# Ten gate tiles moved into the seven-product stage, and the recurrence's setup in longer vector operations

## The chip, the core and the metric

The kernel runs on one core of one Trainium2 chip. The core has five engines with an instruction queue each: PE (TensorE, matmuls), DVE (VectorE), ACT (ScalarE), POOL (GpSimd) and SP (SyncE, which here only starts transfers). They run side by side and wait for each other by semaphores. The metric is the device time of one execution in microseconds, and the median of the runs is what counts.

## What is computed

One layer of a streaming encoder on 512 positions (L) of 2048 channels (D), all in float32:

```
h = rmsnorm(x, norm_g)
[v, bg, cg, za | u, zb | ga, gb] = h @ w_in          # 4x2048 | 2x1024 | 2x2048 columns
ya = bg * causal_conv3(cg * v);   ya = (ya * silu(za)) @ w_out_a
yb = gelu(s5_scan(u, ...));       yb = yb * sigmoid(yb @ w_glu + b_glu)
yb = (yb * silu(zb)) @ w_out_b
m  = sigmoid(ga) * ya + sigmoid(gb) * yb
out = rmsnorm(x + m @ w_o, final_g)
```

`s5_scan` is a diagonal complex recurrence: 64 groups of 16 channels, 64 states each, with a per-state decay that is worked out from a_re, a_im and log_dt.

## The kernel before

**Float32 on PE.** A weight w is split into a rounded w_hi (a cast on ACT, line 544) and w_lo = w - w_hi (a subtraction on DVE, line 561); an activation is held as the same kind of pair. `WStream` loads the weights (128x1024 at a time, w_raw, on SP) some steps ahead and keeps four w_hi and four w_lo buffers. A plain `gemm` is 8 k-steps of three matmuls 128x512: hi times hi, hi times lo, lo times hi (lines 696 to 698), 24 matmuls. An output tile of 128 channels by 512 positions needs two gemms (2048 input channels).

**Stages.** (1) u, the recurrence's input, seven tiles at once (to 98.6 us). (2) The gate stage: tiles of ga, gb and zb, two gemms each, and beside them, as background work, the recurrence. (3) `glu` and w_out_b, and two further ga tiles. (4) The seven-product stage: cg, v, za and bg, two tiles at a time. `seven` multiplies 2x2 blocks (two tiles by two halves of the positions) with seven products instead of eight, a `product` being 8 k-steps of one matmul of 512 columns (line 922) and one of 256 (line 924). Its sums of weights are made by `add7` on DVE. (5) Two last ga tiles, then w_out_a, then w_o. The gates go through tanh on ACT (line 823) and are parked in DRAM (ga_d, gb_d) by POOL until stage 5.

**Background work.** `bg` is a list of generators. `gemm(..., steps=RATE)` advances the list by RATE steps after each gemm. In the gate stage the list holds the recurrence's parameters, then four `Block`s (16 of the 64 groups each), then eight gelu pieces. A Block has a `front` (factors f for every power, small matrices bb, and sl, made by DVE and ACT), `pe1` (float32 matmuls on PE that need sl, line 338, and bb with f, line 347), `post` (mi, el), `scan` on DVE (seven doublings that make the rotations rr and ri, then a turn of h, a scan of 16 instructions at line 415, and a turn back) and `pe2` (matmuls of h with el, lines 430 and 433). `ssm_blocks` runs them in the order front 0, then for each block pe1, pe2 of the block before, post, front of the next, scan.

**What sets the order.** The code is written in one stream. A scheduler then puts each engine's instructions into one fixed queue, and an engine runs its queue in order.

In the changed code the numbers of these lines are 1 to 3 higher, so that line 823 appears as L826 in the order rows of the change, 544 as L545, 561 as L562, 338 as L339, 433 as L434, 325 (sl) as L326.

Of the kernel before, what the change touches and what calls it, by code (L numbers as in the profile page):

```python
# [12 lines left out]
AF = mybir.ActivationFunctionType  # L13
ALU = mybir.AluOpType
ADD, SUB, MUL = ALU.add, ALU.subtract, ALU.mult

P = 128
L = 512
D = 2048
KD = D // P  # L20
NG, NP, NC = 64, 64, 16
NQ = NG // 2
NB = 4
QB = NQ // NB
T = 4
# [1 line left out]
SLOT = 1024  # L27
EPS = 1e-6
MAGIC = 12582912.0
RATE = 2.75  # L30
PRATE = 1.0
WARM = 9
NR4 = 37
NA = 12
NAB = 14
HL = L // 2


# [198 lines left out]
class Block:  # L237
# [13 lines left out]
    def front(self):  # L251
        c, nc, b, q0, msk = self.c, self.c.nc, self.b, self.q0, self.msk
        tt, ts, stt = _ew(nc)
# [19 lines left out]
        cr, ci = smal[:, :, 1, 0, :], smal[:, :, 1, 1, :]  # L273
        shp = [P, QB, NC]
        ft = self.new([P, QB, 5, NC], "ft")
        for ri in range(2):
            f = self.new([P, QB, 5, NC], "f")
            for tau in range(5):
                pr = c.pw[:, tau, 0, q0:q0 + QB].unsqueeze(2).to_broadcast(shp)
                pi = c.pw[:, tau, 1, q0:q0 + QB].unsqueeze(2).to_broadcast(shp)  # L280
                tt(ft[:, :, tau, :], ci, pi if ri == 0 else pr, MUL)
                tt(f[:, :, tau, :], cr, pr if ri == 0 else pi, MUL)
                if tau == 2:
                    yield
            if ri == 0:
                tt(f, f, ft, SUB)
            else:
                fl = f.rearrange("p q t c -> p (q t c)")
                stt(fl, fl, -1.0, ft.rearrange("p q t c -> p (q t c)"), MUL, SUB)
            self.F.append(f)  # L290
            yield
# [21 lines left out]
        tmp = self.new([P, QB, 2, NP], "t")  # L313
        for ri in range(2):
# [8 lines left out]
            m = self.new([P, QB, 2, NP], "sl")  # L323
# [254 lines left out]
def hybrid_kernel(ctx: ExitStack, tc: tile.TileContext, xT, x, cvec, fg, wu, wu7, wabc,  # L578
                  wgz, wgb, wga, wo, par, bs_d, be_d, ce_d, out):
    nc = tc.nc  # L580
    tt, ts, stt = _ew(nc)
    act = nc.scalar
    c = Ctx()
# [16 lines left out]
    def wide(name, shape=(P, 2, L)):  # L600
        t = r4b.tile(list(shape), F32, tag="r4", name=name)
        return t

    def tmp():
        if r4b:
            return wide("tmp")[:, 0]
        t = tp_ctx.tile([P, L], F32, tag="tmp", name="tmp")
        return t
# [9 lines left out]
    W, W2 = WStream(c, 2, 2), WStream(c, 0, 0)  # L618
# [20 lines left out]
    for j in range(0, KD, 2):  # L639
        for i in range(4):  # L640
            W.add7(wabc[j, i, 0], wabc[j + 1, i, 0], wabc[j + 1, i, 1], wabc[j, i, 1])
    for j in range(NAB, KD):
        for h in range(2):
            W.add(wga[j, h])
    for j in range(KD):
# [25 lines left out]
    ga_d = [drp.tile([P, L], F32, name=f"ga{j}") for j in range(KD)]  # L671
    gb_d = [drp.tile([P, L], F32, name=f"gb{j}") for j in range(KD)]
    tb_d = [drp.tile([P, L], F32, name=f"tb{j}") for j in range(KD)]
    uy = uyp_ctx.tile([P, 8, T, NCH], F32, name="uy")


    bg = []
# [115 lines left out]
    yg = []  # L793

    def gelu(m):
        y = uy[:, m].rearrange("p s k -> p k s")
        t, u = tmp(), tmp()
        t3, u3 = (v.rearrange("p (k s) -> p k s", s=T) for v in (t, u))
        act.activation(t3, y, AF.Square)
        ts(t, t, 0.044715, MUL, 1.0, ADD)  # L800
        tt(t3, t3, y, MUL)
        yield
        act.activation(u, t, AF.Tanh, scale=0.7978845608028654)
        stt(t3, u3, 1.0, y, ADD, MUL)
        g = pair()
        split(g, t)
        yg.append(g)
        yield
# [17 lines left out]

    for j in range(NA):
        gate(ga_d[j], RATE)
    for j in range(KD):
        gate(gb_d[j], RATE)  # L830
    zb = []
    for m in range(8):
# [3 lines left out]
        tz = tmp()  # L836
# [91 lines left out]
    def seven(name):  # L928

        o = wide(name)  # L930
        e1, pb = wide("half"), psum()
        product(pb, Y11, True, False)
        act.copy(e1[:, 0], pb)
        e2, pd = wide("half"), psum()
        product(pd, T1, True, False)
        act.copy(e2[:, 1], pd)
        product(pb, T2, False, False)
        act.copy(e1[:, 1], pb)
        product(pd, Y22, False, True)
        tt(e1[:, 1], pd, e1[:, 1], ADD)  # L940
        product(pb, T3, False, False)
        tt(e2[:, 1], pb, e2[:, 1], ADD)
        pa = psum()
        product(pa, Y21, True, True)
        tt(e1[:, 0], pa, e1[:, 0], ADD)
        for i, e in enumerate((e1, e2)):
            if i:
                product(pb, T4, False, True)
                act.copy(e2[:, 0], pb)
            v = e.rearrange("p b (h l) -> p b h l", h=2)  # L950
            tt(o[:, i].rearrange("p (b l) -> p b l", b=2), v[:, :, 0], v[:, :, 1], ADD)
        return o
# [19 lines left out]
    def out_a(cc, b, j):  # L972
        tt(b, b, cc, MUL)
        nc.gpsimd.dma_start(yag_d[j // 2], b)
        yield

    for j in range(0, KD, 2):
        cc = seven("cg")
        v = seven("v")
        bg.append(conv(cc, v, j))  # L980
        z = seven("za")
        bg.append(silu(cc, z))
        b = seven("bg")
        bg.append(out_a(cc, b, j))
    while bg:
        step()

# [14 lines left out]
        bg.append(reload(i))  # L1002
    for _ in range(3):
        step()
    for j in range(NAB, KD):
        gate(ga_d[j], 4.0)
    while bg:
        step()
# [15 lines left out]
    for j in range(KD):  # L1024
# [4 lines left out]
        t = mq[j]  # L1029
        stt(t[:, 0], t[:, 0], 1.0, ps, ADD, MUL)  # L1030
        stt(t[:, 1], t[:, 1], 0.25, t[:, 0], MUL, ADD)
        p = pair()
# [8 lines left out]
    for t in range(4):  # L1041
        for i in range(2):
            o = c.r4.tile([P, 1024], F32, tag="r4", name="o")
# [45 lines left out]
    for t in range(4):  # L1089
# [16 lines left out]
        v, r, s = (st[:, t, i:i + 1] for i in (5, 6, 7))  # L1106
# [92 lines left out]
```

## Time and profile before

| what | value |
|---|---|
| median of 3 runs | 1708.33 us (1706.68 to 1710.23) |
| the profiled execution | 1708.12 us, of which 1706.3 us are the span of the trace |
| PE busy | 1693.8 us, 99% of the span |
| DVE busy | 1202.0 us, 70% |
| ACT busy | 684.9 us, 40% |
| granted TensorE clock | 0.997 |

The span is the time from the first to the last instruction in the trace; 1.8 us lie around it. A row of a timeline gives the start, the duration, engine, line, operation and tiles, and in brackets how long the engine stood idle before it and what ended that. A row of groups gives the count, the busy time with the mean duration in ns, and the idle time before the group's instructions. The matmuls are pipelined: a duration is longer than the distance to the next start.

### The profile page before, as it was taken

How to read it: one execution, taken by the hardware profiler on the slowest of the kernel's cores; microseconds unless marked ns; L12 is line 12 of the kernel's file. 1: busy time of each engine (PE TensorE's matmuls, PEld its weight loads, DVE VectorE, ACT ScalarE, POOL GpSimd, SP SyncE). 2: the span in 40 equal slices, each digit the busy share in tenths (PEclk: the TensorE clock that was granted, in tenths of full speed). 3: DMA queues.
4: the chain of work that ended last, by engine and by line, in shares of the span. 5: the costliest groups of instructions: out<-in, count | busy, mean ns of one | idle time of the engine just before them, and what ended most of it. 6: DMA issues, size and time to landing. Idle time of an engine off the chain costs nothing.

```text
span 1706.3 us, 21911 instructions
## 1 busy us (share of the span) xinstructions
PE 1693.8 (99%) x8516; PEld 1437.5 (84%) x8516; DVE 1202.0 (70%) x1781; ACT 684.9 (40%) x883; POOL 130.4 (8%) x224
## 2 busy tenths in 40 slices
PE   9999999999999999999999999999999999999997
PEld 7888888888888888888888888888888888888887
DVE  7895483939758677598989889888989644333433
ACT  6434423333326422454545544454545422223221
POOL 0003213040100021000000000000000210000000
PEclk9999999999999999999999999999999999999999
DMA  8323335443441453333333332334334943363212
GB/s 300 112 94 125 111 137 124 139 127 122 149 124 50 165 169 136 111 99 112 99 124 120 117 122 99 112 99 132 114 125 141 349 164 112 111 225 121 74 38 99
DMA packets 65256, 221.96 MB, mean 130 GB/s; under 512 B 8896, under 2 KB 9024, under 8 KB 65152
## 3 DMA queue, kind: packets, MB, share of 16 engines
q1 hardware_dynamic: 49392, 170.94, 29.6%
q0 software_dynamic: 15040, 48.53, 9.1%
q8 instruction: 66, 1.08, 0.3%
q10 hardware_dynamic: 720, 1.10, 0.2%
q14 instruction: 38, 0.31, 0.1%
HBM read 195.24 MB, written 21.10 MB: 127 GB/s over the span
## 4 chain that ended last, share of the span: by engine, by line
PE 98%; DMA 1%; DVE 0%; ACT 0%; SPq 0%; issue 0%; DVEq 0%
PE ps L922 25%; PE ps L698 15%; PE ps L696 15%; PE ps L697 15%; PE ps L924 12%; PE ps L1054 3%; PE ps L1052 3%; PE ps L1053 3%; PE ps L773 1%; PE ps L774 1%; PE ps L775 1%; PE ps L433 1%; PE ps L338 1%; PE ps L347 1%; PE ps L430 0%; DMA w_raw<-in_wu_dram 0%
## 5 line engine op out<-in xcount | busy, mean ns | idle before, releaser
L544 ACT CAST w_hi<-w_raw 128x1024 fp32r<-128x1024 f32 (+2 forms) x341 | 355.8, 1044 | 696.0 <-PE ps L697 352.3
L561 DVE TENSOR_TENSOR w_lo<-w_raw,w_hi 128x1024 fp32r<-128x1024 f32 (+2 forms) x341 | 412.1, 1212 | 310.1 <-ACT w_hi L544 305.9
L696 PE MATMUL ps<-pair,w_hi 128*128 128x512 f32 x1104 | 431.1, 391 | 0.0
L698 PE MATMUL ps<-pair,w_lo 128*128 128x512 f32 x1104 | 429.8, 390 | 0.6 <-DVE w_lo L561 0.6
L697 PE MATMUL ps<-pair,w_hi 128*128 128x512 f32 x1104 | 430.1, 390 | 0.0
L922 PE MATMUL ps<-h_comb,w_hi 128*128 128x512 f32 x1024 | 366.2, 399 | 0.0
L924 PE MATMUL ps<-h_comb,w_lo 128*128 128x256 f32 x1024 | 288.2, 281 | 0.0
L922 PE MATMUL ps<-pair,w_hi 128*128 128x512 f32 x768 | 275.7, 399 | 0.0
L698 PEld LDWEIGHTS ps<-pair,w_lo 128*128 128x128 f32 x1104 | 207.4, 188 | 43.9 <-DVE w_lo L561 1.1
L696 PEld LDWEIGHTS ps<-pair,w_hi 128*128 128x128 f32 x1104 | 207.5, 188 | 42.4
L697 PEld LDWEIGHTS ps<-pair,w_hi 128*128 128x128 f32 x1104 | 207.4, 188 | 42.4
L922 PEld LDWEIGHTS ps<-h_comb,w_hi 128*128 128x128 f32 x1024 | 192.8, 188 | 47.6
L924 PE MATMUL ps<-pair,w_lo 128*128 128x256 f32 x768 | 216.1, 281 | 0.0
L924 PEld LDWEIGHTS ps<-h_comb,w_lo 128*128 128x128 f32 x1024 | 194.0, 189 | 0.0
L922 PEld LDWEIGHTS ps<-pair,w_hi 128*128 128x128 f32 x768 | 144.6, 188 | 35.7
L924 PEld LDWEIGHTS ps<-pair,w_lo 128*128 128x128 f32 x768 | 145.5, 189 | 0.0
L544 ACT CAST w_hi<-w_sum 128x1024 fp32r<-128x1024 f32 x64 | 67.4, 1053 | 104.4 <-PE ps L922 94.1
L561 DVE TENSOR_TENSOR w_lo<-w_sum,w_hi 128x1024 fp32r<-128x1024 f32 x64 | 78.0, 1219 | 7.2 <-ACT w_hi L544 7.2
L1052 PE MATMUL ps<-w_hi,pair 128*128 128x512 f32 (+1 forms) x212 | 81.8, 386 | 0.0
L1053 PE MATMUL ps<-w_lo,pair 128*128 128x512 f32 (+1 forms) x212 | 81.7, 386 | 0.0
L1054 PE MATMUL ps<-w_hi,pair 128*128 128x512 f32 (+1 forms) x212 | 81.7, 386 | 0.0
L47 DVE TENSOR_TENSOR half<-ps,half 128x512 f32<-128x512 f32 x96 | 65.6, 683 | 1.9 <-PE ps L924 1.9
(189 smaller groups left out, 1697.8 us busy)
## 6 DMA issues: line engine op xcount, KB each, us to landing
w_raw<-in_wabc_dram SPq DMA_DIRECT2D x128, 512.0 KB, 3.8
w_raw<-in_wga_dram SPq DMA_DIRECT2D x64, 512.0 KB, 3.6
w_raw<-in_wgb_dram SPq DMA_DIRECT2D x48, 512.0 KB, 4.0
w_raw<-in_wo_dram SPq DMA_DIRECT2D x32, 512.0 KB, 3.3
w_raw<-in_wgz_dram SPq DMA_DIRECT2D x24, 512.0 KB, 3.6
w_raw<-in_wu_dram SPq DMA_DIRECT2D x15, 448.0 KB, 7.7
xt<-in_xT_dram SPq DMA_DIRECT2D x16, 256.0 KB, 6.8
ga<-tmp POOLq DMA_DIRECT2D x16, 256.0 KB, 2.3
```

The costliest lines, as they stand in the source:

```text
L47: return v.tensor_tensor(out=o, in0=a, in1=b, op=op)
L338: nc.tensor.matmul(ps[:, i * NCH:(i + 1) * NCH], self.sl[ri][:, q].rearrange("p g s -> p (g s)"), self.u4[:, q, :], start=True, stop=True)
L544: nc.scalar.copy(hi[:, a:b], raw[:, a:b])
L561: nc.vector.tensor_tensor(out=lo[:, a:b], in0=raw[:, a:b], in1=hi.bitcast(F32)[:, a:b], op=SUB)
L696: nc.tensor.matmul(ps, hi[:, k], a[:, 0], start=first and k == 0, stop=False)
L697: nc.tensor.matmul(ps, hi[:, k], a[:, 1], start=False, stop=False)
L698: nc.tensor.matmul(ps, lo[:, k], a[:, 0], start=False, stop=last and k == 7)
L922: nc.tensor.matmul(both, hi[:, k], a, start=first and k == 0, stop=False, skip_group_check=True)
L924: nc.tensor.matmul(both[:, 1], lo[:, k], a[:, 0], start=False, stop=last and k == 7, skip_group_check=True)
L1052: nc.tensor.matmul(ps, a[:, 0, cs], hi[:, k2, c0:c1], start=first and k2 == 0, stop=False)
L1053: nc.tensor.matmul(ps, a[:, 0, cs], lo[:, k2, c0:c1], start=False, stop=False)
L1054: nc.tensor.matmul(ps, a[:, 1, cs], hi[:, k2, c0:c1], start=False, stop=last and k2 == 1)
```

## The change

Three things change.

1. The first part makes 2 ga tiles instead of 12 (NA), stage 3 makes tiles 2 and 3 (NA to NAB). Tiles 4 to 13 are made as five pairs by `seven("ga")` in the seven-product stage, one pair after each of the rounds j = 2, 4, 6, 8 and 10; a new `gate2` takes tanh of both tiles in one ACT operation of 128x1024 and sends two halves to ga_d on POOL. Tiles 14 and 15 stay where they were (NB7 = 14). As the gate stage has 52 gemms now and not 72, RATE goes from 2.75 to 3.8 steps per gemm: the same 198 steps in all.
2. `Block.front` makes its products for all five powers in one operation of 128x640 with broadcast operands, not in five of 128x128: 4 operations for 20.
3. `gelu` first copies its strided input into a contiguous tile on ACT; the operations after it read that tile.

```diff
-RATE = 2.75
+RATE = 3.8
-NA = 12
-NAB = 14
+NA = 2
+NAB = 4
+NB7 = 14
...
         for ri in range(2):
-            f = self.new([P, QB, 5, NC], "f")
-            for tau in range(5):
-                pr = c.pw[:, tau, 0, q0:q0 + QB].unsqueeze(2).to_broadcast(shp)
-                pi = c.pw[:, tau, 1, q0:q0 + QB].unsqueeze(2).to_broadcast(shp)
-                tt(ft[:, :, tau, :], ci, pi if ri == 0 else pr, MUL)
-                tt(f[:, :, tau, :], cr, pr if ri == 0 else pi, MUL)
-                if tau == 2:
-                    yield
+            f = self.new(sh5, "f")
+            tt(ft, c5[1], p5[1 - ri], MUL)
+            tt(f, c5[0], p5[ri], MUL)
+            yield
...
             W.add7(wabc[j, i, 0], wabc[j + 1, i, 0], wabc[j + 1, i, 1], wabc[j, i, 1])
-    for j in range(NAB, KD):
+        i = NAB + j - 2
+        if NAB <= i < NB7:
+            W.add7(wga[i, 0], wga[i + 1, 0], wga[i + 1, 1], wga[i, 1])
+    for j in range(NB7, KD):
...
     def gelu(m):
-        y = uy[:, m].rearrange("p s k -> p k s")
-        t, u = tmp(), tmp()
-        t3, u3 = (v.rearrange("p (k s) -> p k s", s=T) for v in (t, u))
-        act.activation(t3, y, AF.Square)
+        y, t, u = tmp(), tmp(), tmp()
+        act.copy(y.rearrange("p (k s) -> p k s", s=T), uy[:, m].rearrange("p s k -> p k s"))
+        act.activation(t, y, AF.Square)
         ts(t, t, 0.044715, MUL, 1.0, ADD)
-        tt(t3, t3, y, MUL)
+        tt(t, t, y, MUL)
         yield
         act.activation(u, t, AF.Tanh, scale=0.7978845608028654)
-        stt(t3, u3, 1.0, y, ADD, MUL)
+        stt(t, u, 1.0, y, ADD, MUL)
...
+    def gate2(o, j):
+        t = wide("tz")
+        act.activation(t, o, AF.Tanh, scale=0.5)
+        for i in range(2):
+            nc.gpsimd.dma_start(ga_d[j + i], t[:, i])
+        yield
...
         bg.append(out_a(cc, b, j))
+        i = NAB + j - 2
+        if NAB <= i < NB7:
+            bg.append(gate2(seven("ga"), i))
...
-    for j in range(NAB, KD):
+    for j in range(NB7, KD):
         gate(ga_d[j], 4.0)
```

The scheduler gives other queues for this, in the gate stage above all. Two places follow, both in that stage.

*ACT, up to the matrices sl of block 2.* `tmp<-ps` is the tanh of a finished gate tile and waits for the last matmul into that ps; `w_hi<-w_raw` is the cast that a later gemm needs. Before, where the tile after ps_2496 is ps_2590 and reads w_hi_2439 and w_hi_2499:

```order
L544 CAST w_hi_2439<-w_raw_2329 128x1024
L823 ACTIVATE tmp_2493<-ps_2393 128x512
L544 CAST w_hi_2499<-w_raw_2394 128x1024
L823 ACTIVATE tmp_2587<-ps_2496 128x512
L544 CAST w_hi_2538<-w_raw_2437 128x1024
L544 CAST w_hi_2593<-w_raw_2497 128x1024
L325 ACTIVATE ssm_sl_2530<-ssm_t_2527,cvec_t_75 128x8x64 x2
L308 COPY ssm_bb_2479<-ssm_ft_2424 64x32x16 x2
L308 COPY ssm_bb_2480<-ssm_ft_2424 64x32x16 x2
```

In the change, where the tile after ps_2304 is ps_2394 and reads w_hi_2249 and w_hi_2307:

```order
L545 CAST w_hi_2143<-w_raw_2031 128x1024
L545 CAST w_hi_2198<-w_raw_2079 128x1024
L826 ACTIVATE tmp_2192<-ps_2078 128x512
L826 ACTIVATE tmp_2301<-ps_2195 128x512
L826 ACTIVATE tmp_2391<-ps_2304 128x512
L545 CAST w_hi_2249<-w_raw_2141 128x1024
L326 ACTIVATE ssm_sl_2226<-ssm_t_2189,cvec_t_75 128x8x64 x2
L545 CAST w_hi_2307<-w_raw_2196 128x1024
L309 COPY ssm_bb_2175<-ssm_ft_2136 64x32x16 x2
L309 COPY ssm_bb_2176<-ssm_ft_2136 64x32x16 x2
L326 ACTIVATE ssm_sl_2232<-ssm_t_2189,cvec_t_75 128x8x64 x2
```

Casts and tanhs alternated, and both casts for a tile stood ahead of the tanh of the tile before it. Now three tanhs stand in a row, and both casts for ps_2394 stand behind the tanh of ps_2304. Block 3's rows in the change are the same, with other buffer numbers. Right behind these sl, PE has pe1 of block 2 and then, some four gemms on, pe2 of block 1.

*PE, from the gemm ahead of block 0's pe1.* Before, with the 48 matmuls into ps_1482 (two gemms) cut to the first and the last:

```order
L697 MATMUL ps_1384<-pair_868,w_hi_1274 128x512
L698 MATMUL ps_1384<-pair_868,w_lo_1327 128x512
L696 MATMUL ps_1482<-pair_619,w_hi_1325 128x512
...
L698 MATMUL ps_1482<-pair_868,w_lo_1431 128x512
L338 MATMUL ps_1553<-ssm_u4_1354,ssm_sl_1513 128x128 x4
L338 MATMUL ps_1559<-ssm_u4_1354,ssm_sl_1513 128x128 x4
L338 MATMUL ps_1566<-ssm_u4_1354,ssm_sl_1519 128x128 x4
L696 MATMUL ps_1575<-pair_619,w_hi_1429 128x512
```

In the change:

```order
L701 MATMUL ps_1411<-pair_868,w_hi_1319 128x512
L702 MATMUL ps_1411<-pair_868,w_lo_1370 128x512
L339 MATMUL ps_1443<-ssm_u4_1290,ssm_sl_1399 128x128 x4
L339 MATMUL ps_1449<-ssm_u4_1290,ssm_sl_1399 128x128 x4
L339 MATMUL ps_1456<-ssm_u4_1290,ssm_sl_1405 128x128 x4
L339 MATMUL ps_1462<-ssm_u4_1290,ssm_sl_1405 128x128 x4
L348 MATMUL ps_1498<-ssm_f_1310,ssm_bb_1352 128x64
```

On ACT, the tanh that stands last ahead of sl_1513 before is that of ps_1384; the last one ahead of sl_1399 in the change is that of ps_1411, with one cast between it and sl. Two gemms lay between that tile and pe1, and there are none now.

More of the change, by code (lines that the diff above doesn't have):

```diff
@@ L275, in front @@
         ft = self.new([P, QB, 5, NC], "ft")
+        sh5 = [P, QB, 5, NC]
+        p5 = [c.pw[:, :, i, q0:q0 + QB].rearrange("p t q -> p q t").unsqueeze(3).to_broadcast(sh5)
+              for i in range(2)]
+        c5 = [v.unsqueeze(2).to_broadcast(sh5) for v in (cr, ci)]
         for ri in range(2):
-            f = self.new([P, QB, 5, NC], "f")
-            for tau in range(5):
-                pr = c.pw[:, tau, 0, q0:q0 + QB].unsqueeze(2).to_broadcast(shp)
-                pi = c.pw[:, tau, 1, q0:q0 + QB].unsqueeze(2).to_broadcast(shp)
-                tt(ft[:, :, tau, :], ci, pi if ri == 0 else pr, MUL)
-                tt(f[:, :, tau, :], cr, pr if ri == 0 else pi, MUL)
-                if tau == 2:
-                    yield
+            f = self.new(sh5, "f")
+            tt(ft, c5[1], p5[1 - ri], MUL)
+            tt(f, c5[0], p5[ri], MUL)
+            yield
             if ri == 0:
```

## The prediction, written before the changed kernel was run

> **What bounds the kernel now.** I read the page first, then what PE waited for, then the stages one by one.
>
> ```profile
> span 1706.3 us, 21911 instructions
> ...
> PE 1693.8 (99%) x8516; PEld 1437.5 (84%) x8516; DVE 1202.0 (70%) x1781; ACT 684.9 (40%) x883; POOL 130.4 (8%) x224
> ...
> PE 98%; DMA 1%; DVE 0%; ACT 0%; SPq 0%; issue 0%; DVEq 0%
> ...
> L698 PE MATMUL ps<-pair,w_lo 128*128 128x512 f32 x1104 | 429.8, 390 | 0.6 <-DVE w_lo L561 0.6
> ```
>
> PE is busy for 99% of the span and is 98% of the chain that ended last; in all plain gemms it waited 0.6 us. So every microsecond of matmul taken away counts, and so does every wait that PE does not have today. The windows by stage (busy us of PE, PEld, DVE, ACT, POOL) show what stands beside it:
>
> ```profile
> 99.60:490.00 390.40, 390.15 (x1923) 330.85 (x1924) 268.88 (x641) 136.70 (x193) 76.87 (x121) 1.00 0.40 125
> ...
> 693.70:1010.00 316.30, 316.30 (x1792) 274.69 (x1791) 278.41 (x284) 157.45 (x188) 2.15 (x4) 1.00 0.35 111
> ```
>
> In the gate stage (first row) DVE is busy 69% of the time, in the seven-product stage (second row) 88%, and PE stands still in neither.
>
> **What the move takes away.** A plain gemm is 24 matmuls. Two casts to w_hi, each released by the last L697 of a gemm, give its length:
>
> ```profile
> 143.02 1.05 ACT L544 CAST w_hi<-w_raw 128x1024 fp32r<-128x1024 f32 x1 [4.38 <-PE ps L697]
> ...
> 148.46 1.05 ACT L544 CAST w_hi<-w_raw 128x1024 fp32r<-128x1024 f32 x1 [3.89 <-PE ps L697]
> ```
>
> 5.44 us, 0.227 per matmul, so a pair of gate tiles (four gemms) costs 21.76. One `seven` is 7 products of 16 matmuls; the second window above has 1792 of them in 316.30 us, which makes 19.77 per `seven`. Five pairs: 5 x 1.99 = **9.9 us less** on PE. Their 20 loads become 20 loads, their 20 casts and 20 w_lo become 35 each, with four sums per pair, in a stage where DVE has 12% and ACT half of its time free; I cost that at nothing: DVE's work there hides behind PE, and rival 4 says what it costs if it does not. On SP the same 20 loads of 512 KB only change places; on POOL ten transfers to ga move into a stage in which POOL has 2 us of work per 316.
>
> **What the change adds: waits of PE in the gate stage.** The background work (the recurrence, then gelu) is spread over 52 gemms instead of 72. On average it fits. DVE would have 268.88 less 20 w_lo and a little of the front, about 242 us, in some 333 us (52 x 5.44, and about 50 us of small matmuls). But the queues are fixed orders, and the two places in the order rows show what decides. Prices first, from ACT's timeline around block 0's matrices, and from one cast and the matmul that releases it:
>
> ```profile
> 154.13 0.60 ACT L823 ACTIVATE tmp<-ps 128x512 f32<-128x512 f32 x1 [4.61 <-PE ps L698]
> 154.62 1.05 ACT L544 CAST w_hi<-w_raw 128x1024 fp32r<-128x1024 f32 x1
> 158.06 1.34 ACT L325 ACTIVATE ssm_sl<-ssm_t,cvec_t 128x512 f32<-128x512 f32 x2 [2.40 <-DVE ssm_t L47]
> 159.31 2.50 ACT L308 COPY ssm_bb<-ssm_ft 64x512 f32<-64x512 f32 x4
> 161.83 1.05 ACT L544 CAST w_hi<-w_raw 128x1024 fp32r<-128x1024 f32 x1
> 162.79 1.33 ACT L325 ACTIVATE ssm_sl<-ssm_t,cvec_t 128x512 f32<-128x512 f32 x2
> ```
> ```profile
> 98.13 0.39 PE L697 MATMUL ps<-pair,w_hi 128*128 128x512 f32 x1
> ```
> ```profile
> 98.60 1.05 ACT L544 CAST w_hi<-w_raw 128x1024 fp32r<-128x1024 f32 x1 [4.38 <-PE ps L697]
> ```
>
> A reader of PE's result starts 0.47 us after the matmul's start. A tanh holds ACT for 0.49 before the next instruction starts, a cast for 0.96, a pair of sl takes 1.33, four bb copies 2.52.
>
> *Block 0, pe1.* Before, PE had the gemms into ps_1482 between the tanh that precedes sl and pe1. Now pe1 follows directly on the gemm whose tanh stands ahead of the cast and of sl: 0.47 + 0.49 + 0.96 + 1.33 = 3.25 us after the last L698 starts, where PE could go on after 0.23. Wait 3.0. The second sl is there 4.72 us after the first (159.40 to 164.12 in the rows), and PE has only eight small matmuls for it. Their length, and that of pe2's 24:
>
> ```profile
> 164.81 2.84 PE L338 MATMUL ps<-ssm_u,ssm_sl 128*128 128x128 f32 x24
> 167.40 0.48 PE L696 MATMUL ps<-pair,w_hi 128*128 128x512 f32 x1
> 343.98 0.44 PE L430 MATMUL ps<-ssm_u,ssm_mi 128*128 128x128 f32 x2
> ...
> 349.31 0.48 PE L696 MATMUL ps<-pair,w_hi 128*128 128x512 f32 x1
> ```
>
> These float32 matmuls leave two records each: 12 in 2.59 us, 24 in 5.33, so 0.22. Wait 4.72 - 1.8 = 2.9. Together 5.9 us.
>
> [...] If ACT could pass a waiting tanh, the 0.96 us here and 0.96 in each of blocks 1 and 2 below would fall away, and the sum would be 2.9 us lower.
>
> *Blocks 1 and 2, the late cast* (named after the blocks whose pe2 follows; sl are those of blocks 2 and 3). Three tanhs stand in a row ahead of the cast to w_hi_2249, which PE needs for the next gemm at once. The last of them waits for the gemm just running: 0.47 + 0.49 + 1.05 - 0.23 = 1.8 us of waiting. After two matmuls (0.45) PE needs sl, 1.25 after the cast: 0.8 more.
>
> *Blocks 1 and 2, pe2.* With that cast DVE has lost its lead as well. What it has to do before pe2 may start:
>
> ```profile
> 301.93 0.17 DVE L47 TENSOR_TENSOR ssm_rr<-ssm_rr,ssm_keep 128x8 f32<-128x8 f32 x1
> ...
> 302.16 1.22 DVE L561 TENSOR_TENSOR w_lo<-w_raw,w_hi 128x1024 fp32r<-128x1024 f32 x1
> ...
> 307.22 1.21 DVE L561 TENSOR_TENSOR w_lo<-w_raw,w_hi 128x1024 fp32r<-128x1024 f32 x1
> ...
> 310.77 1.23 DVE L561 TENSOR_TENSOR w_lo<-w_raw,w_hi 128x1024 fp32r<-128x1024 f32 x1
> ...
> 316.56 1.22 DVE L561 TENSOR_TENSOR w_lo<-w_raw,w_hi 128x1024 fp32r<-128x1024 f32 x1
> 317.70 2.35 DVE L47 TENSOR_TENSOR ssm_t<-ssm_h,ssm_ri 128x1024 f32<-128x1024 f32 x2
> ...
> 334.10 2.36 DVE L47 TENSOR_TENSOR ssm_h<-ssm_h,ssm_t 128x1024 f32<-128x1024 f32 x2
> 336.37 3.50 DVE L561 TENSOR_TENSOR w_lo<-w_raw,w_hi 128x1024 fp32r<-128x1024 f32 x3
> ```
>
> Here the seven doublings run from 301.93 to 316.56, with three w_lo of 1.14 between them: 11.2 us. Turn, scan and turn run from 317.70 to 336.37: 18.7, 17.5 until the first of the two results. Pe2 came at 343.98, 7.6 us later, so nothing waited; the w_lo for the gemm in between had been ready at 317.7. Now, counted from the end of the late cast: DVE waits for sl (1.25), one half operation (0.6), w_lo 1.14, another 0.6, w_lo 1.14, doublings 11.2, two w_lo 2.3, 17.5: 35.7. PE: 0.45, wait 0.8, eight small ones 1.8, then 98 matmuls (22.2) and 26 small ones (5.7): 31.0. Wait 4.7, and 0.7 for the second result. With the head, 1.8 + 0.8 + 4.7 + 0.7 = 8.0 per block, twice: **16.0**. For block 0 the same count gives PE 30.5 (101 matmuls, 34 small) against DVE 27.9: hidden, with 2.6 to spare.
>
> *Block 3.* Counted from the end of block 2's wait: DVE has seven w_lo 8.0, doublings 11.2, 17.5, and the y and zb operations of these rows:
>
> ```profile
> 258.19 1.12 DVE L55 SCALAR_TENSOR_TENSOR ssm_y<-ssm_u,cvec_t,ps 128x128 f32<-128x128 f32 x4 [5.07 <-PE ps L433]
> ```
> ```profile
> L55 DVE SCALAR_TENSOR_TENSOR zb<-tmp,ps 128x512 f32<-128x512 f32 x3 | 2.0, 680 | 0.1
> ```
>
> Eight y 2.1, four zb 2.4, together 41.2. PE has 148 matmuls and 21 small ones, 38.2. Wait 3.0.
>
> *Front and gelu.* The five 128x128 products become one of 128x640; gelu's strided reading (L799) becomes a copy, and the square then takes what the contiguous tanh (L803) takes:
>
> ```profile
> 150.69 0.28 DVE L47 TENSOR_TENSOR ssm_ft<-ssm_bc,ssm_keep 128x128 f32<-128x128 f32 x1
> ...
> 152.91 0.82 DVE L47 TENSOR_TENSOR ssm_f<-ssm_f,ssm_ft 128x640 f32<-128x640 f32 x1
> 153.65 0.29 DVE L47 TENSOR_TENSOR ssm_f<-ssm_bc,ssm_keep 128x128 f32<-128x128 f32 x1
> ```
> ```profile
> L799 ACT ACTIVATE tmp<-uy 128x512 f32<-128x512 f32 x6 | 6.9, 1152 | 3.1 <-DMA uy<-ssm_y 3.1
> ...
> L803 ACT ACTIVATE tmp<-tmp 128x512 f32<-128x512 f32 x5 | 3.2, 634 | 3.4 <-DVE tmp L47 3.4
> ```
>
> Eleven start in 2.22 us, 0.20 each; one of 640 takes 0.74. No row has the broadcast form, so it lies between 0.74 and 5 x 0.20 = 1.0: 0 to 1.1 us of DVE per block. It stands ahead of sl, and sl waits on ACT for the tanh, so I take no gain (at most 4.3). Gelu pays one more ACT operation of 0.63 (the strided reading, 1.15, moves to the copy) and DVE saves. Where a gemm covers it that is nothing; before `glu` the last two are uncovered: 1.3 (0 to 5.0 for all eight).
>
> **Sum.** 5.9 + 16.0 + 3.0 + 1.3 = 26.2 us of waits. After a rest PE also starts slowly; the program's own start shows how much:
>
> ```profile
> 4.92 0.78 PE L773 MATMUL ps<-pair,w_hi 128*128 128x512 f32 x1
> ...
> 7.20 0.39 PE L775 MATMUL ps<-pair,w_lo 128*128 128x512 f32 x1
> ```
>
> Six matmuls in 2.28 us instead of 1.36: 0.9, taken twice, for the two waits of 5 us: 1.8 (0 to 3.7 with block 0's). The profiled execution took 1708.12 us, 0.2 under the median of the runs: 1708.1 - 9.9 + 26.2 + 1.8 = **1726 us**.
>
> **Rivals.** (1) *Faster, 1698 us (0.12).* The waits do not form, because the work fits on average (242 of 333 us on DVE); only the 9.9 us are left. It decides if the casts keep a lead of one gemm on PE. For it: DVE is idle 31% of the stage today. Against it: the three tanhs in a row. (2) *Only ACT's waits are real (0.17).* DVE's stretch stays hidden as at 336.37 to 343.98, and 5.9 + 2 x 2.6 + 1.3 = 12.4 us stay: 1710.6. (3) *The clock drops (0.12).* [...] (4) *The seven-product stage pays (0.07).* Its pool has six buffers, and gate2 holds one of them for a tanh and two transfers to ga:
>
> ```profile
> ga<-tmp POOLq DMA_DIRECT2D x16, 256.0 KB, 2.3
> ```
>
> If each pair waits for one landing, 5 x 2.3 = 11.5 more: 1738.
>
> **How the numbers follow.** My forecast has 0.52; its own range, from the stretch's margin of 3 us either way at three blocks and the bounds above, is 1717 to 1734. The range to hold 8 of 10 takes in (2) and (3) and part of (4): 1707 to 1735. About 0.2% is what a measurement here can tell from no change (1704.9 to 1711.7). Faster: (1) and the low side of (2), 0.14. Within: most of (2), 0.10. Slower: 0.76.
>
> **What would show it.** Waits of PE on ssm_sl (L339) near 150 us of 3 us twice; on w_hi ahead of blocks 1 and 2; on ssm_h (L434) of about 5 us twice; a seven-product stage that is 98.9 us longer with no new wait; a gate stage shorter by 108.8 and longer by the waits. If PE has no wait on ssm_h, the stretch's price was wrong, and (2) holds; if it has none on ssm_sl either, (1).

## The result, and the profile after

The changed kernel took **1732.56 us** (median of 4 runs, 1730.66 to 1736.53) against 1708.36 us for the kernel before on the same chip: a ratio of 1.0148, 95% interval 1.0136 to 1.0161. It is 24 us slower. The forecast was 1726 us, in a range of 1707 to 1735.

Three lines of the page of the changed kernel stand first: the span, the busy time of the engines, and the share of each engine in the chain that ended last.

```profile
span 1728.9 us, 22111 instructions
...
PE 1694.0 (98%) x8596; PEld 1439.2 (83%) x8596; DVE 1245.0 (72%) x1777; ACT 712.4 (41%) x921; POOL 130.5 (8%) x224
...
PE 82%; DVE 7%; ACT 1%; issue 1%; DMA 1%; POOL 0%; DVEq 0%; ACTq 0%; POOLq 0%
```

PE was 98% of the chain and is 82% now. DVE took 7% of it, where it had none. What PE waited for, in the changed kernel (total, times, longest, in us):

```profile
PE ps L434 <- DVE ssm_h L48: 8.1, 3, 3.1
PE ps L700 <- ACT pair L616: 4.9, 2, 3.1
PE ps L339 <- ACT ssm_sl L326: 4.9, 4, 2.9
PE ps L700 <- ACT w_hi L545: 3.2, 2, 1.6
...
PE ps L701 <- DVE pair L48: 0.8, 1, 0.8
```

None of these five lines has a counterpart before. They add up to 21.9 us, all ahead of the seven-product stage. The windows of that stage, first before, then after, then in a second profiled execution of the changed kernel (run e12 below). The columns are window, length, busy us of PE, PEld, DVE, ACT and POOL with their counts, the granted clock, the busy share of the DMA engines and GB/s:

```profile
693.70:1326.90 633.20, 633.20 (x3586) 549.77 (x3585) 558.14 (x570) 314.89 (x376) 5.88 (x11) 1.00 0.36 117
```
```profile
620.80:1349.50 728.70, 728.70 (x4146) 634.44 (x4145) 636.67 (x650) 366.11 (x436) 11.29 (x21) 1.00 0.36 119
```
```profile
619.20:1351.30 732.10, 732.10 (x4146) 634.84 (x4145) 637.40 (x650) 366.22 (x436) 11.29 (x21) 1.00 0.36 119
```

PE is busy throughout in each. The stage is 95.5 us longer in the first profiled execution and 98.9 in the second, and 5 x 19.77 = 98.9 was forecast. The 3.4 us between the two are taken up in the last section.

**Where the time went, place by place.** A wait is not the whole loss at a place, since PE may also run slowly behind it. So the loss is taken from the starts of PE's matmuls: the distance from one start to the next, less what the same matmul takes in undisturbed stretches (0.227 us for 512 columns, 0.112 for each record of a small float32 one). These are the rows of the changed kernel at the places named in the prediction:

```profile
155.74 3.67 PE L339 MATMUL ps<-ssm_u,ssm_sl 128*128 128x128 f32 x16 [2.85 <-ACT ssm_sl L326]
160.43 2.05 PE L339 MATMUL ps<-ssm_u,ssm_sl 128*128 128x128 f32 x16 [1.03 <-ACT ssm_sl L326]
...
267.40 0.50 PE L700 MATMUL ps<-pair,w_hi 128*128 128x512 f32 x1 [1.62 <-ACT w_hi L545]
268.63 3.62 PE L339 MATMUL ps<-ssm_u,ssm_sl 128*128 128x128 f32 x16 [0.49 <-ACT ssm_sl L326]
...
303.45 1.93 PE L434 MATMUL ps<-ssm_h,ssm_el 128*128 128x127 f32 x6 [3.11 <-DVE ssm_h L48]
...
463.84 0.49 PE L700 MATMUL ps<-pair,w_hi 128*128 128x512 f32 x1 [1.77 <-ACT pair L616]
465.18 0.50 PE L701 MATMUL ps<-pair,w_hi 128*128 128x512 f32 x1 [0.85 <-DVE pair L48]
...
469.06 1.22 PE L700 MATMUL ps<-pair,w_hi 128*128 128x512 f32 x2 [3.14 <-ACT pair L616]
```

The first and fourth row show the slow running, at a granted clock of 0.50 (from 155.89 to 159.30 and from 268.53 to 271.94 us): 16 records of 0.112 should take 1.8 us, and their busy time is 3.67 and 3.62. In the second row the same 16 take 2.05 (the last end is modelled longer). Summed by place, in us, each good to about 0.3:

| place | forecast | changed kernel | second execution |
|---|---|---|---|
| block 0, pe1 on sl | 5.9 | 5.7 | 5.9 |
| block 0, pe2 | 0 | 0 | 0 |
| head of block 1 (cast, then sl) | 2.6 | 4.0 | 2.45 |
| block 1, pe2 on h | 5.4 | 6.35 | 7.7 |
| head of block 2 | 2.6 | 4.1 | 4.1 |
| block 2, pe2 on h | 5.4 | 5.1 | 5.1 |
| block 3, pe2 on h | 3.0 | 2.0 | 1.95 |
| before glu | 1.3 | 8.4 | 7.6 |
| slow restart | 1.8 | in the rows above | in the rows above |
| sum | 28.0 | 35.7 | 34.8 |

With it the profiled execution closes: 1708.1 - 108.8 (20 plain gemms less) + 95.5 + 35.7 = 1730.5 us, and it took 1730.66.

### The profile page after: what moved, and what is told of

It reads as the page before. It is cut to its first block, busy times and chain, and to the rows that moved or that the text cites. A ratio compares the mean times of both kernels' runs of the same rounds, so it can differ in the third digit from the quotient of the medians.

```text
span 1728.9 us, 22111 instructions
## 1 busy us (share of the span) xinstructions
PE 1694.0 (98%) x8596; PEld 1439.2 (83%) x8596; DVE 1245.0 (72%) x1777; ACT 712.4 (41%) x921; POOL 130.5 (8%) x224
## 4 chain that ended last, share of the span: by engine, by line
PE 82%; DVE 7%; ACT 1%; issue 1%; DMA 1%; POOL 0%; DVEq 0%; ACTq 0%; POOLq 0%
PE ps L925 28%; PE ps L927 14%; PE ps L700 9%; PE ps L702 9%; PE ps L701 9%; PE ps L1065 3%; PE ps L1067 3%; PE ps L1066 3%; DVE ssm_t L48 2%; DVE ssm_h L48 1%; PE ps L434 1%; DVE ssm_h L416 1%; DVE w_lo L562 1%; DVE ssm_rr L48 1%; DMA uy<-ssm_y 1%
## 5 line engine op out<-in xcount | busy, mean ns | idle before, releaser
L925 PE MATMUL ps<-h_comb,w_hi 128*128 128x512 f32 x1184 | 421.4, 397 | 0.0
L700 PE MATMUL ps<-pair,w_hi 128*128 128x512 f32 x944 | 368.8, 392 | 8.1 <-ACT pair L616 4.9
L702 PE MATMUL ps<-pair,w_lo 128*128 128x512 f32 x944 | 368.1, 391 | 0.7 <-DVE w_lo L562 0.7
L701 PE MATMUL ps<-pair,w_hi 128*128 128x512 f32 x944 | 367.9, 390 | 0.8 <-DVE pair L48 0.8
L927 PE MATMUL ps<-h_comb,w_lo 128*128 128x256 f32 x1184 | 332.3, 281 | 0.0
L925 PE MATMUL ps<-pair,w_hi 128*128 128x512 f32 x888 | 317.1, 397 | 0.0
L925 PEld LDWEIGHTS ps<-h_comb,w_hi 128*128 128x128 f32 x1184 | 222.2, 188 | 54.0 <-DVE half L48 0.4
L927 PE MATMUL ps<-pair,w_lo 128*128 128x256 f32 x888 | 249.2, 281 | 0.0
L927 PEld LDWEIGHTS ps<-h_comb,w_lo 128*128 128x128 f32 x1184 | 223.7, 189 | 0.0
L700 PEld LDWEIGHTS ps<-pair,w_hi 128*128 128x128 f32 x944 | 177.8, 189 | 46.1 <-ACT pair L616 5.8
L701 PEld LDWEIGHTS ps<-pair,w_hi 128*128 128x128 f32 x944 | 178.0, 189 | 37.8 <-DVE pair L48 1.2
L925 PEld LDWEIGHTS ps<-pair,w_hi 128*128 128x128 f32 x888 | 166.6, 188 | 40.2
L545 ACT CAST w_hi<-w_sum 128x1024 fp32r<-128x1024 f32 x74 | 78.0, 1054 | 122.4 <-PE ps L925 95.6
L562 DVE TENSOR_TENSOR w_lo<-w_sum,w_hi 128x1024 fp32r<-128x1024 f32 x74 | 90.2, 1219 | 7.2 <-ACT w_hi L545 7.2
```

The source lines that it names most:

```text
L545: nc.scalar.copy(hi[:, a:b], raw[:, a:b])
L562: nc.vector.tensor_tensor(out=lo[:, a:b], in0=raw[:, a:b], in1=hi.bitcast(F32)[:, a:b], op=SUB)
L700: nc.tensor.matmul(ps, hi[:, k], a[:, 0], start=first and k == 0, stop=False)
L701: nc.tensor.matmul(ps, hi[:, k], a[:, 1], start=False, stop=False)
L702: nc.tensor.matmul(ps, lo[:, k], a[:, 0], start=False, stop=last and k == 7)
L925: nc.tensor.matmul(both, hi[:, k], a, start=first and k == 0, stop=False, skip_group_check=True)
```

## The experiments

**Which part costs it.** Three kernels: before with its RATE alone changed, the move alone (old front, old gelu), and the new front and gelu alone (no tile moved).

```diff
# e1: before
-RATE = 2.75
+RATE = 3.8
# e2: the changed kernel, with Block.front and gelu as before
-            tt(ft, c5[1], p5[1 - ri], MUL)
-            tt(f, c5[0], p5[ri], MUL)
+            for tau in range(5):
...
# e3: before, with Block.front and gelu of the change
```

> The kernel before with nothing changed but RATE 3.8 instead of 2.75: all twelve gate tiles stay in the first part, and the background work is squeezed into the first 52 gemms as the change squeezes it. Theory 'squeeze' (the loss comes from the denser background work, and PE then waits in the gate stage and pays a slow clock after each wait): 1735 to 1750 us, with PE waits on ssm_sl, w_hi and ssm_h at about 150, 265, 300, 345 and 380 us, and no wait before glu. Theory 'move' (the loss comes from the gate pairs in the seven-product stage or from the new operations): 1708 us, no new waits.

> The change without its new front and its new gelu: only the ten tiles moved and RATE 3.8. 'Squeeze': 1733 to 1742 us, at least as slow as the change, since the old front keeps DVE busier ahead of each scan (about 1 us per block). 'New operations' (the front's broadcasts or gelu's copy cost): about 1715 to 1725 us. 'Seven-product stage': 1732 us as well, with its waits there.

> The kernel before with the new front and the new gelu alone, no tile moved, RATE 2.75. 'Squeeze': 1707 to 1709 us, because nothing on the path changes while the gate stage has cover. 'New operations': 1712 us or more.

Measured: e1 1745.38 us, ratio 1.0221 (1.0201 to 1.0241). e2 1742.16 us, 1.0204 (1.0189 to 1.0219), 0.2 us above its range. e3 1707.4 us, 0.9999 (0.9987 to 1.0011). What PE waited for in e1 and in e2:

```profile
PE ps L433 <- DVE ssm_h L47: 13.6, 6, 5.5
PE ps L338 <- ACT ssm_sl L325: 4.8, 3, 3.8
PE ps L696 <- ACT w_hi L544: 3.2, 2, 1.6
```
```profile
PE ps L434 <- DVE ssm_h L48: 12.2, 5, 4.0
PE ps L339 <- ACT ssm_sl L326: 4.8, 3, 3.8
PE ps L700 <- ACT w_hi L545: 3.2, 2, 1.6
PE ps L700 <- ACT pair L616: 2.4, 4, 0.9
```

In e1 not one tile has moved and not one operation has been added; the steps alone come faster. The waits on sl, on the cast and on h are there, and PE loses 35.8 us in the gate stage by the same count of starts. So the squeeze makes these waits, not the moved tiles. What e1 does not have is the wait before glu: its background work ends some 20 gemms early. In e2 that wait is there, and PE loses 45.4 us. In e3 the new front is worth nothing, because nothing waits.

**The front or gelu.** The changed kernel with the old gelu, so that against e2 only the front differs, and against the change only gelu:

```diff
     def gelu(m):
-        y, t, u = tmp(), tmp(), tmp()
-        act.copy(y.rearrange("p (k s) -> p k s", s=T), uy[:, m].rearrange("p s k -> p k s"))
-        act.activation(t, y, AF.Square)
+        y = uy[:, m].rearrange("p s k -> p k s")
...
+        act.activation(t3, y, AF.Square)
...
```

> The change with the old gelu (the new front kept). Together the old front and old gelu made the change 9.6 us slower. 'The front counts' (it shortens DVE's work ahead of each scan, so the waits on ssm_h shrink at blocks 0 to 2): 1733 to 1736 us, ssm_h waits as in the change (8 us in all), only the waits before glu differ. 'Gelu counts': 1739 to 1742 us, with ssm_h waits as in the change but more before glu.

Measured: 1734.1 us, 1.0159 (1.0146 to 1.0173). PE loses 35.7 us in the gate stage, as in the changed kernel, 8.4 of them before glu. So the new gelu neither costs nor saves anything that can be seen, and the new front takes 9.7 us off the loss (45.4 to 35.7): 8 us of run time in a stage where DVE and the path to sl set PE's pace, and nothing in e3, where they do not. PE's wait on h in e7, to be set beside that of e2:

```profile
PE ps L434 <- DVE ssm_h L48: 7.9, 3, 3.1
```

The waits on h fall from 12.2 to 7.9 us, those on sl do not fall (4.8 and 5.0). The rest of the 9.7 is slow running that went with the longer waits: the granted clock stood at half for 41 us of e2's gate stage and for 27 of e7's. One row of groups in the gate stage of the changed kernel gives the new front's price:

```profile
L48 DVE TENSOR_TENSOR ssm_f<-ssm_bc,ssm_keep 128x640 f32<-128x640 f32 x8 | 6.2, 819 | 0.0
```

A broadcast product of 128x640 takes 0.82 us, like the plain one in the prediction's rows (0.82), which was the cheaper of the two bounds.

**The order of the queues.** e4 places pe2 of a block behind the front of the next block but one, so that PE comes for h later:

```diff
     for i, k in enumerate(blocks):
         yield from k.pe1()
-        if i:
-            yield from blocks[i - 1].pe2()
         yield from k.post()
         if i + 1 < n:
             yield from blocks[i + 1].front()
+        if i:
+            yield from blocks[i - 1].pe2()
         yield from k.scan()
```

> The change with one edit in the order of the recurrence: pe2 of the block before comes after the next block's front, not straight after pe1. 'Squeeze, by the order of the queues': the waits on ssm_h at 303 and 381 us fall from 3.1 to under 1 us, those on w_hi and sl ahead of blocks 2 and 3 go, the slow clock at 268, 304, 346 and 384 us goes with them: 1711 to 1719 us. 'Squeeze, by the amount of work' (DVE cannot do it in 52 gemms wherever pe2 stands): waits of the same sum elsewhere, 1728 to 1735 us.

Measured: 1719.62 us, 1.0072 (1.0057 to 1.0087), 0.6 us above its range. The waits of PE:

```profile
PE ps L339 <- ACT ssm_sl L326: 5.5, 2, 2.9
PE ps L434 <- DVE ssm_h L48: 5.2, 5, 2.0
PE ps L700 <- ACT pair L616: 3.1, 1, 3.1
```

The line for the cast is gone, and the longest wait on h is 2.0 instead of 3.1. The wait on sl, which lies ahead of every pe2, stays, and so does one before glu (the last line). Same tiles, same operations, 13 us less: so half of the 24 us is a matter of order, and not of background work that does not fit into 52 gemms. For the other half this run leaves that open.

**Fewer pairs, with and without the order.** e6 moves three pairs and changes nothing else. e5 moves three pairs, has pe2 late as in e4, and four empty steps ahead of block 0's pe1, so that the tanh and the sl behind it are done when PE comes.

```diff
# e6, to the changed kernel
-RATE = 3.8
+RATE = 3.3
-NA = 2
-NAB = 4
+NA = 6
+NAB = 8
# e5: RATE 3.45, NA and NAB as in e6, pe2 as in e4, and
     yield from blocks[0].front()
+    for _ in range(4):
+        yield
```

> Three pairs moved (NA 6), RATE 3.3 so that the same number of steps is spread over 60 gemms; nothing else of the change touched. If the loss grows in proportion to what is moved: 3/5 of 24 = 14 us over the kernel before. 'Squeeze, by the order of the queues': the waits are few places that appear or not; by the order of this kernel's queues only block 0's sl (3 us), about 2 us before the last pe2 and 2.5 us before glu are left, with two slow spells: 2 to 6 us over the kernel before.

> Three pairs moved instead of five (NA 6, so 60 gemms stay in the gate stage), RATE 3.45, pe2 after the next block's front, and four empty steps between block 0's front and its pe1. 'Squeeze, by the order of the queues': no wait of PE in the gate stage is left, and the three pairs give 3 x 1.99 = 6.0 us: 5 to 6 us under the kernel before (ratio 0.9965 to 0.997). 'Seven-product pairs give nothing': ratio 1.000. 'Any squeeze costs': at least 5 us over the kernel before.

Measured: e6 1717.93 us, 1.0058 (1.0043 to 1.0073), against 1706.62 for the kernel before: 11.3 us more. That lies between the two expectations and bears out neither alone. Its losses are 4.25 us at block 0's pe1, 7.85 before glu, and 2.4 at the pe2s: the first two keep most of their price, the pe2s lose most of theirs (13.45 in the table), and the heads of blocks 1 and 2 cost nothing. e5 took **1702.23 us, 0.9965 (0.9951 to 0.9978)**. Its waits:

```profile
PE ps L702 <- ACT pair L618: 0.8, 1, 0.8
PE ps L704 <- DVE w_lo L564: 0.7, 1, 0.7
```

No wait on sl, h or a cast is left. The profiled span is 1700.1 us against 1706.3, 6.2 less; the medians differ by 4.4, and the ratio makes 6.0. Three pairs at 1.99 make 6.0. The seven-product stage shows the size most closely:

```profile
628.00:1320.70 692.70, 692.70 (x3922) 600.62 (x3921) 605.49 (x618) 345.76 (x412) 9.16 (x17) 1.00 0.36 118
```

That is 59.5 us more than the 633.2 of before, where 3 x 19.77 = 59.3 was forecast. The saving by the seven products is real and was sized rightly.

**Does the slow clock cost what it seems to?** e8 adds 12 small float32 matmuls (24 records, of which nobody reads the result) ahead of pe2 of blocks 1 and 2, so that PE is at work while it waits for h:

```diff
+FILL = 12
...
+        self.t0 = t0
...
+        if self.b in (1, 2):
+            fp = c.psum()
+            for i in range(FILL):
+                nc.tensor.matmul(fp[:, :NCH], u4[:, i % QB, :], self.t0[:, i % QB, :], start=True, stop=True)
```

> The change with twelve small matmuls (2.7 us, into a PSUM tile that nothing reads) put ahead of pe2 of blocks 1 and 2, on an operand that DVE finishes some 5.7 us before h: PE works through most of the 3.1 us for which it waited on ssm_h. 'The clock is a cost of its own': the slow spells at 302.7 to 309.5 and 381 to 384.5 us go, and with them 3.4 and 1.7 us: 1726 to 1729 us. 'The clock only follows the waits and costs nothing beside them': 1732 us, or up to 1736 where the extra matmuls delay pe2.

Measured: 1730.5 us, 1.0136 (1.0122 to 1.0149), 2 us under the changed kernel, with intervals that overlap. The PE rows at block 1's pe2:

```profile
298.37 2.94 PE L431 MATMUL ps<-ssm_t,ssm_u 128*128 128x128 f32 x24 [1.44 <-DVE ssm_t L49]
...
302.91 0.71 PE L440 MATMUL ps<-ssm_h,ssm_el 128*128 128x127 f32 x4 [0.23 <-DVE ssm_h L49]
```

The matmuls run at full speed now, yet pe2's first matmul on h starts at 302.91 instead of 303.45. DVE is done with h when it is, and PE that was fast merely waits. By places PE loses 25.5 us instead of 35.7, and the filler itself takes 48 x 0.112 = 5.4: between 4 and 5 us are left as a gain in the gate stage. In the profiled execution of e8 the seven-product stage gave them back: it took 733.7 us, 1.6 more than e12's 732.1 (one wait of 1.3 on half) and 5.0 more than the changed kernel's 728.7. In total the result lies between the two expectations, and no more than that can be read from it. The filler is also not the only difference: the heads of blocks 1 and 2, which stand ahead of their block's filler, ran at full speed too. The window of the clock's grid in which their waits fell held 1.79 us of work (see the last section), so this is a matter of when they fell, as at block 1 in e12. At the four places together (two heads, two pe2s) some 8 us of slow running are gone, and with the filler's own 5.4 counted between 3 and 4 us are gained: a slow stretch ahead of a wait for DVE is partly paid by that wait.

**What is fixed by the queues, and what is not.** e12 is the changed kernel once more.

> The changed kernel itself, a second execution under the profile, for what is fixed by the queues and what is not. In the changed kernel the waits at the head of block 1 (1.6 and 0.5 us) were followed by half clock and cost 4.0 us, while the kernel with the two tiles ahead of glu lost 2.45 us at the same place with the same waits, and 1.5 us more at the pe2 that follows. Theory (whether a short rest brings half clock depends on when it falls, and a loss ahead of pe2 is given back there, since pe2 waits for DVE): the heads cost 2.45 or about 4.0, a head and its pe2 together 9 to 10.5 us whichever it is, and the half-clock spells need not stand where they stood. The seven-product stage takes 731 to 732 us, as in all the other kernels with five pairs, and not 728.7. Rival (the waits alone decide): the same spells at the same places, the heads 4.0 and 4.1, and pe2 6.3 and 5.1.

Measured: 1732.9 us, 1.015 (1.0127 to 1.0173). The rows at the head of block 1 and at its pe2:

```profile
266.92 0.50 PE L700 MATMUL ps<-pair,w_hi 128*128 128x512 f32 x1 [1.62 <-ACT w_hi L545]
268.15 2.05 PE L339 MATMUL ps<-ssm_u,ssm_sl 128*128 128x128 f32 x16 [0.50 <-ACT ssm_sl L326]
...
302.97 1.93 PE L434 MATMUL ps<-ssm_h,ssm_el 128*128 128x127 f32 x6 [4.62 <-DVE ssm_h L48]
```

The waits at the head are the same 1.62 and 0.50 us, but here the 16 matmuls behind them run at full speed (2.05 us busy instead of 3.62). The head costs 2.45 instead of 4.0, PE reaches pe2 1.5 us earlier and waits 4.62 instead of 3.11. Head and pe2 together cost 10.2 us here and 10.4 there. The seven-product stage took 732.1 us, as expected but for 0.1. So the theory holds: the slow stretch is a matter of when a rest falls, and ahead of a wait for DVE it is given back.

**The wait before glu.** e9 sets the two ga tiles that stood between w_out_b and the seven-product stage between the last zb tile and glu, as cover for the last gelu pieces:

```diff
...
     while bg:
         step()
+    for j in range(NA, NAB):
+        gate(ga_d[j])
     yb = []
...
-        gemm(ps, yb, steps=1.2)
+        gemm(ps, yb, steps=1.5)
...
-    for j in range(NA, NAB):
-        gate(ga_d[j], 2.0)
```

> The changed kernel, but the two ga tiles that stood between w_out_b and the seven-product stage stand between the last zb tile and glu (four gemms, 21.8 us, no background step in them; the steps beside w_out_b go from 1.2 to 1.5 per gemm for what they carried). The gate stage itself keeps its order. In the changed kernel PE loses 8.4 us at glu's first gemm (waits 5.8, the rest at half clock). Theory (the last gelu pieces are merely late, as the stage is over when their steps are): the four gemms cover them, the 8.4 us go, and at most 3 to 5 us come back at the start of the seven-product stage, whose first sums of weights then have no tiles ahead of them: 1724 to 1729, no wait of PE on a pair. Rival (the gelu pieces are slow by themselves and take DVE's time from the casts wherever they stand): 5 us or more of waits stay in or behind the four gemms: 1731 to 1736.

Measured: 1735.32 us, 1.016 (1.014 to 1.0179). The theory fell, and the rival's range held. The profiled execution is the fastest of the four, 1728.98 us where the others took 1735.22 to 1738.52; the last section shows where it gained, behind the places read here. ACT's queue, and the PE matmul that waits for it, in the four gemms that were to be the cover:

```profile
468.92 1.11 ACT L801 COPY tmp<-uy 128x512 f32<-128x512 f32 x1
...
470.59 0.60 ACT L616 CAST pair<-tmp 128x512 fp32r<-128x512 f32 x1
471.10 0.59 ACT L840 ACTIVATE tmp<-ps 128x512 f32<-128x512 f32 x1
471.59 1.03 ACT L545 CAST w_hi<-w_raw 128x1024 fp32r<-128x1024 f32 x1
```
```profile
472.67 0.80 PE L700 MATMUL ps<-pair,w_hi 128*128 128x512 f32 x1 [2.87 <-ACT w_hi L545]
```

No matmul waits for a pair any more. But the cast that the covering gemm needs stands behind these gelu operations in ACT's queue, and PE waits 2.87 us for that; with the slow stretch the place still costs 6.3 us, and 3.5 more come at the start of the seven-product stage, whose first sums of weights have lost their cover. So a gemm covers the tail of gelu only where its cast is ahead of that tail.

**Four pairs.** e10 is e5 with four pairs, the tiles of stage 3 set ahead of glu as in e9, though with steps, so that the gate stage keeps 60 gemms. e11 keeps one tile in stage 3 and has 58 gemms.

```diff
# e10, to e5
-NA = 6
-NAB = 8
+NA = 4
+NAB = 6
# with the calls moved as in e9, at RATE
# e11, to e5
-RATE = 3.45
+RATE = 3.65
-NA = 6
-NAB = 8
+NA = 5
+NAB = 6
-    for _ in range(4):
+    for _ in range(6):
         yield
```

> Four pairs in the seven-product stage: the kernel of three pairs with pe2 later and four empty steps ahead of pe1 (1702.2), with two ga tiles fewer in the first part, and the two tiles of stage 3 set ahead of glu, with steps, so that the gate stage keeps 60 gemms at 3.45 steps. Theory (what counts is the number of gemms beside the background work, and stage 3 can do without its tiles): 4 x 1.99 = 7.9 us gained, 3 to 5 us lost at the start of the seven-product stage as in the kernel above: 1701.5 to 1704. If nothing is lost there: 1698 to 1700. Rival (waits come back in the gate stage or at glu): above 1706.

> Four pairs again, with the gate stage at 58 gemms (five ga tiles instead of six in the kernel of three pairs), 3.65 steps per gemm and six empty steps ahead of block 0's pe1, and one ga tile left between w_out_b and the seven-product stage, so that its first sums of weights have 10.9 us ahead of them. If the order of the queues is what counts, nothing is lost in the gate stage and nothing, or under 1.5 us, at the start of the seven-product stage: 1706.6 - 7.9 = 1698.7, so 1698 to 1700.5. If two gemms fewer beside the background work bring waits back, or one tile is not enough: 1702 or above.

Measured: e10 1702.09 us, 0.9969 (0.9957 to 0.9981), inside its first range; in its profile PE loses some 4 us at the start of the seven-product stage, as the expectation has it. e11 1701.7 us, 0.9973 (0.9963 to 0.9983), 1.2 us above the range of its theory and short of the rival's. In its profile the gate stage loses 2.0 us, and its span is 6.5 us under that of before, where four pairs should give 7.9. e5, e10 and e11 cannot be told apart. All three beat the kernel before by some 4.5 us, and the changed kernel by 30. The fourth pair gives about what it costs.

## Why the prediction was right, and where it was not

**Direction and range: right.** Slower had 0.76, and 1732.56 lies in the range of 1707 to 1735. It is 6.6 us above the forecast, and just under the top of the forecast's own range (1734).

**"Five pairs, 9.9 us less": right.** 98.9 us in e12 against the 108.8 of 20 plain gemms, and e5's stage for three pairs agrees (59.5 for 59.3).

**Casts, sums and transfers of the seven-product stage at nothing: right.** PE is busy for the whole of each window quoted, with DVE at 87%; rival 4 is out.

**Block 0's pe1, 5.9: right in the sum**, 5.7 and 5.9, but not wait for wait. The first wait is there (2.85 us of standing still). Of the second, forecast at 2.9, only 1.03 are left, because PE ran its small matmuls slowly meanwhile (16 of them in 3.67 us at a granted clock of 0.50). In e4, where the clock fell later (0.50 from 160.15 us on, against 155.89), both waits stand nearly in full (2.9 and 2.6), and with the slow running behind them the place costs some 7.5. That the sum came out at 5.9 all the same is partly luck: slow running, which the forecast did not have here, filled the second wait.

**The late cast, 2.6 per block: right** (2.45) where the granted clock stayed at 1.00, 4.0 where it went to 0.50.

**Blocks 1 and 2, pe2: the count of DVE's stretch was right.** It gave a wait of 4.7 us. The second execution has 4.62 at block 1, behind a head without a slow stretch, and e9's longest wait on h is 4.6 as well; elsewhere the slow head has taken 1.5 of it, and 3.1 are left. Rival 2, in which that stretch stays hidden, is out. "Hidden, with 2.6 to spare" held for block 0's pe2, thanks to the new front: e2, with the old one, loses 4.5 us there. Block 3 was put at 3.0 and cost 2.0.

**"The front: I take no gain (at most 4.3)" was too low.** The change as a whole was priced with its own queues, so the sum does not suffer. But the front is worth 8 us in this stage (e2 to e7). The waits on h fall by 4.3, which is the bound; what the bound leaves out is the slow running behind those waits. The waits on sl do not fall, as the prediction had it.

**The term that was mis-sized most is "before glu the last two are uncovered: 1.3".** It cost 8.4 and 7.6 us. The step priced one more ACT operation per piece, and e7 shows that this operation is not the matter. What it left out is the length of the whole tail: a gelu piece goes to and fro between ACT and DVE three times, and each of the eight k-steps of a glu gemm needs a piece of its own. ACT's first gelu operation before and after, each followed by the summary of all eight (count, shortest, middle and longest duration in ns, first and last start in us):

```profile
507.45 1.14 ACT L799 ACTIVATE tmp<-uy 128x512 f32<-128x512 f32 x1 [3.10 <-DMA uy<-ssm_y]
...
L799 ACT ACTIVATE tmp<-uy x8: 1121/1136/1256, 507.4 to 535.0; 128x512 f32<-128x512 f32 x8
```
```profile
445.79 1.13 ACT L801 COPY tmp<-uy 128x512 f32<-128x512 f32 x1 [6.60 <-DMA uy<-ssm_y]
...
L801 ACT COPY tmp<-uy x8: 1074/1124/1146, 445.8 to 474.4; 128x512 f32<-128x512 f32 x8
```

The eight pieces start over some 28 us in both kernels, and both tails begin when the last y has landed in uy. Glu's first matmul stands 28 gemms (672 matmuls) ahead of the seven-product stage. Counted back, that is at 541.4 us before, 34 us after 507.45 and with all eight pieces begun. After, it is at 459.9, 14 us after 445.79. PE goes through the pieces that are ready, stands from 461.9 for a piece whose cast ends at 463.79, and then for the next, whose cast ends at 469.0. The recurrence's last block had lost 20 us of lead, and no row of the prediction followed it to the end of the stage.

**"Slow PE restart, 1.8" was right in kind and far too small.** In the changed kernel slow matmuls make some 11.6 us of the 35.7: 1.2, 1.6, 3.1, 1.7, 1.9 and 2.1 at six of the places of the table. Rival 3, the clock that drops (0.12), is borne out in kind: the granted clock was 0.50 for 27.3 us of the changed kernel's gate stage, in six spells at these six places. But no run shows one price per rest (1.2 to 3.1 us here), and the length of a rest alone did not decide it (last section). Nor do the 11.6 us add to the waits of the forecast: part of them lies inside waits for DVE and ACT (block 0's pe1 costs 5.7 with a slow stretch that does its work while sl is still being made). Against the 28.0 forecast, glu explains 7.1 us, the slow heads 2.9, block 1's pe2 0.95; the other places give 1.5 back, and the 1.8 for restarts are in these rows already: 7.7 in all. The profiled execution's faster seven-product stage took 3.4 off again.

**Rival 1, 1698 without any wait, is out for the change as it stands.** A gate stage without waits on sl, h or a cast is seen only in e5 and e10, with the order put right, three and four pairs moved, and 60 gemms left; e11, with 58, loses 2.0 us again. Whether the work can be fitted into 52 gemms without waits stays open: no run has five pairs and no waits, and e4, the nearest, is still 13 us above the kernel before.

## What to carry to other kernels

When cover is taken away from background work, read the average for whether it can fit, and the order of the queues for what it costs: here tanhs that wait ahead of casts and of sl (block 0's pe1 and the two heads, 13.8 us) cost as much as the waits for DVE's h (13.45). Follow the background to its end as well: count how much lead its last piece has over the first matmul that needs it. Losses at neighbouring waits are not added blindly: a slow or late stretch ahead of a wait for another engine shortens that wait (here 4.62 us to 3.11), so a repair is priced at the end of the chain and not at the place repaired.

## What the hardware showed that was not expected

**In these traces the granted clock changes on a fixed grid.** In the changed kernel it dropped from 1.00 to 0.50 at 155.89, 268.53, 302.66, 347.03, 381.17 and 466.50 us. All the distances between these times are multiples of 3.413 us, to within 0.03, and each spell of 0.50 lasted 3.41 or 6.83 us. In the second execution the grid has another offset. Windows on each grid, first of the changed kernel, then of the second execution (window, length, busy us of PE with the count, clock, DMA share, GB/s):

```profile
265.11:268.53 3.42, 1.40 (x5) 1.00 0.20 77
268.53:271.94 3.41, 3.31 (x15) 0.50 0.03 5
...
299.25:302.66 3.41, 1.09 (x5) 1.00 0.48 150
302.66:306.07 3.41, 2.62 (x11) 0.50 0.65 234
```
```profile
264.26:267.68 3.42, 1.77 (x7) 1.00 0.09 37
267.68:271.09 3.41, 2.94 (x21) 1.00 0.10 40
...
298.40:301.81 3.41, 0.00 (x0) 1.00 0.46 142
301.81:305.22 3.41, 2.25 (x9) 0.50 0.59 210
```

The window in which PE was busy for 1.40 us was followed by one at half clock; the one with 1.77 was not. Over the nine profiles with slow stretches in the gate stage (both executions of the changed kernel, e1, e2, e4, e6, e7, e8, e9), each window of the grid showed 1.00 or 0.50. Every full-clock window of that stage with up to 1.52 us of work was followed by half clock, none with 2.06 or more was, and between 1.62 and 1.87 both happened. Every slow window with up to 2.82 us of work was followed by another slow one, and none with 2.98 or more was. So the same rest of 1.62 and 0.50 us fell into one window at 265.11, and was split over two at 264.26 and 267.68: the head cost 4.0 us once and 2.45 once. Here the length of a rest did not decide alone.

**A faster pace, unexplained.** In the changed kernel's profile the seven-product stage ran 1.9% faster for a while, behind a hitch of 0.1 us at 1013.6:

```profile
1013.50:1187.40 173.90, 173.90 (x1003) 153.14 (x1003) 156.24 (x161) 88.98 (x106) 2.15 (x4) 1.00 0.36 118
```

That is 0.1734 us per matmul where the whole stage before has 633.20 / 3586 = 0.1766, at the same granted clock. The second execution has none of it (732.10 / 4146 = 0.1766). It makes the 3.4 us between the two executions. The profile of e9 has it for longer, again behind a hitch (a wait of PE near 627 us) and up to the next one:

```profile
640.60:990.00 349.40, 349.40 (x2017) 308.11 (x2016) 313.82 (x322) 178.92 (x213) 4.31 (x8) 1.00 0.36 118
```

That is 0.1732 per matmul, and at 0.1766 this window alone would have taken 6.8 us more, which is about what sets that execution apart from the other three of e9. A hitch is not enough for it: e8 has one near 909 us, and its pace stays as it was (733.7 us for the stage, 0.1767 per matmul without its wait of 1.3). No run tested what causes it, and it stays open.
